# A fused decoder layer on one core: order of the additions, weight loads and first feed-forward products between cross-attention and the feed-forward part

## The chip, the cores and the metric

The kernel runs on one NeuronCore of a Trainium2 chip as one launch. The metric is the device time of that launch in microseconds (us). Three runs of the kernel before gave 2944.31, 2949.00 and 2949.56 us; the median, 2949.0 us, is the time before. Engines are called by the names of the profile: PE (TensorE), DVE (VectorE), ACT (ScalarE), POOL (GpSimd), SP (SyncE, which here only issues DMAs).

## The reference, cut to what matters

One decoder layer is applied to 512 prompt tokens and to 8 x 4 sample tokens, which share the weights. All values are float32.

```
x = x + concat(stick_breaking_attention, gated_delta_net) @ w_out
hx = rmsnorm(x, norm_x_g)
xq = rmsnorm(hx @ w_xq per head, x_q_norm_g)            # 4 heads of 128
attn = softmax(xq . mem_k / sqrt(128))                  # 256 memory tokens
x = x + (attn @ mem_v) @ w_xo                           # w_xo: 512 x 2048
hf = rmsnorm(x, norm_ffn_g)
gate, up = split(hf @ w_gate_up)                        # 2048 x 2*5632
x = x + (silu(gate) * up) @ w_down                      # 5632 x 2048
```

The prompt attends to memory keys and values computed from `mem_prompt`, the samples to cached ones (`cache_mem_k`, `cache_mem_v`). The change lies at the seam between the last two additions: the product with `w_xo`, the norm `norm_ffn_g`, and the first products with `w_gate_up`.

## The kernel before

**Layout.** Features lie on the partitions. The token vector `x` is 16 tiles (blocks) of 128 features x 544 tokens; the 544 tokens are worked on in two halves of 272 columns. A product of float32 numbers is made of three matmuls: both factors are split into a high and a low part (`wh`/`wl` for a weight, `xh`/`xl` or the two parts of `pr` for the tokens), and high x high, high x low and low x high are added in PSUM. The high part is made by a cast on ACT, the low part by a subtraction on DVE.

**Cross-attention** (`cross`, L1522). Side work for the sample tokens (`cross_sample`, L1434) runs between the projections: it loads cached keys (`xk`, L1456) in two halves and then cached values (`xv`, L1465) in four groups of four tiles, all on SP. Then the product with `w_xo` runs in two parts, one for each half of the tokens. Each part has 16 blocks, each block 12 matmuls (L1570) into a PSUM tile `mm` (two of them exist). The weights of one block (four 128 x 128 tiles, 256 KB) are loaded by one DMA (`wxo`, L1546, through `weights`, L191) into a raw tile `wr` (three exist), cast (L203) and subtracted (L204). The first six blocks are kept for part 1; the other ten are loaded again, two blocks ahead. After a block's matmuls DVE adds the PSUM tile to `x` (L1573).

**The operands of the feed-forward part.** Two blocks of `x` make a `Pair`. `Pair.first` and `Pair.second` multiply by the norm's gain (`gain`, partly on POOL, L1635, partly on ACT, L1637), `sums` makes four differences and sums on DVE (L1666 to L1669, tiles `v`), and `make` splits them into parts `pr` (cast L1640 on ACT, subtraction L1641 on DVE). In parallel `Stats` squares `x` (ACT, L266) and accumulates `acc` on POOL (L267). `Stats.rstd` (L270) then sums `acc` over the partitions with a matmul (L277) into PSUM and makes `rstd2` out of it and of `r1`, the earlier norm's factor (L281, L282, then a logarithm and an exponential on ACT). `aux` is one PSUM tile here, so the second half's matmul waits until DVE has read the first half's.

**The feed-forward part** uses a scheme of seven products in place of eight. One product (`Ffn.product`, L2006) is 24 matmuls of 272 columns; the kernel calls it a tick. What every engine does is written out by hand: `Work.at(tick, place, do)` enters a step in a list, and `Work.run` (L1702) emits each tick's steps by their place. Steps of the ticks below 0, and those of ticks 0 to 4 with a place under 70, get a higher priority in the scheduler, so that they may move ahead of the part before. There are two sets of PSUM banks for gate and up. One set (`gu_banks[0]`) shares its PSUM space with `mm`, the other one (`gu_banks[1]`) has its own.

`FirstGateUp` (L1798) runs the first pair of hidden columns as eight products in ticks 0 to 7. Its raw weight tiles (512 KB each, `raw`) are loaded by SP, cast on ACT (L1785) and subtracted on DVE (L1789). `open` (L2015) starts four accumulators with one matmul each. `scale` calls `rstd` for `rstd2`, both halves, in tick 5. `unscale` (L2020 to L2030) runs in tick 20: it transposes `rstd2`, multiplies `r1` by it (L2029) and takes the reciprocal of all 128 x 544 elements (L2030), which POOL uses from tick 41 on.

Each engine executes its instructions in the order in which they stand; the order comes from the scheduler, which goes by the steps' priorities.

Of the kernel before, what the change touches and what calls it, by code (L numbers as in the profile page):

```python
# [12 lines left out]
ALU = mybir.AluOpType  # L13
# [239 lines left out]
class Stats:  # L253
# [16 lines left out]
    def rstd(self, name, scale=None):  # L270

        c, nc = self.c, self.c.nc
        r = c.cst.tile([P, T], F32, tag="rstd", name=name, bufs=2)
        for h in range(2):
            cols = slice(h * HT, (h + 1) * HT)
            ps = c.aux()
            nc.tensor.matmul(ps[:, :HT], c.ones, self.acc[:, cols], start=True, stop=True)  # L277
            if scale is None:
                rsq(c, r[:, cols], ps[:, :HT], 1.0 / D)
                continue  # L280
            nc.vector.tensor_mul(r[:, cols], scale[:, cols], scale[:, cols])  # L281
            nc.vector.scalar_tensor_tensor(r[:, cols], r[:, cols], D * EPS, ps[:, :HT], ALU.mult, ALU.add)  # L282
            rsq(c, r[:, cols], r[:, cols], 1.0 / D, eps=c.zero)
        return r
# [1148 lines left out]
def cross_sample(c, qs, outs, scale, tiles):  # L1433
# [14 lines left out]
    yield 0.3, 2.5  # L1448
    for h2 in range(2):

        def load(b, i):
            if h2 or b >= 2:
                t = c.tt("xk")[:, :512]
            else:
                t = c.pb.tile([P, 4, P], F32, tag="wh", name="xk", bufs=XO_KEPT).rearrange("p k m -> p (k m)")
            nc.sync.dma_start(  # L1456
                t.rearrange("p (a h d) -> p a h d", a=2, h=2), c.cache_mk[0, b, :, h2 * 2 : h2 * 2 + 2].rearrange("(a p) h d -> p a h d", p=P)
            )
            return t

        ps = yield from sample_logits(c, f, h2 * 2, load, 1, ps if h2 else None, h2 * 256)

    def loadv(b, j):
        t = c.act.tile([P, T], F32, tag=("ah", "al")[b % 2], name="xv", bufs=KD)[:, :512]
        nc.sync.dma_start(t, c.cache_mv[0, b, j * P : (j + 1) * P].rearrange("p h d -> p (h d)"))  # L1465
        return t


    values = [[loadv(i // 2 * 4 + b, i % 2) for b in range(4)] for i in range(3)]
# [22 lines left out]
    for half in range(2):  # L1492
        ps = c.aux()
        for j in range(2):
# [7 lines left out]
            if not half and not j:  # L1502
                values.append([loadv(4 + b, 1) for b in range(4)])
# [17 lines left out]
def cross(c, acts, st, x, side):  # L1521
# [24 lines left out]
    def wxo(m):  # L1546
        if m < len(kept):
            return kept[m]
        if len(kept) == XO_KEPT:
            return weights(c, c.w_xo, 0, 4, m * P)  # L1550
        kept.append(weights(c, c.w_xo, 0, 4, m * P, kept=True))
        return kept[-1]

    for part in range(2):
# [4 lines left out]
        ahead = [wxo(m) for m in range(2)]  # L1559
        for m in range(KD):  # L1560
            ps = c.mm()
            if m + 2 < KD:
                with c.tc.high_priority(PRIO):
                    ahead.append(wxo(m + 2))
# [7 lines left out]
            with c.tc.high_priority(100):  # L1572
                nc.vector.tensor_add(x[m][:, cols], x[m][:, cols], ps[:, 0, :HT])  # L1573
# [222 lines left out]
class FirstGateUp:  # L1796
# [3 lines left out]
    def __init__(self, f):  # L1800
        self.f, self.c, self.cols, self.a, self.hi, self.lo = f, f.c, (0, HID), {}, {}, {}
        at = f.work.at
        (A, B, C, _), (A1, B1, C1, _) = f.gu_banks
# [156 lines left out]
class Ffn:  # L1960
# [4 lines left out]
    def __init__(self, c, pairs, st, r1):  # L1965
# [13 lines left out]
        at(0, 1, self.open)  # L1979
        at(5, 35, self.scale)  # L1980
        at(20, 35, self.unscale)
        self.xq = c.dram.tile([KD, P, T], F32, name="xq")
# [27 lines left out]
    def open(self):  # L2010

        g = self.first
        for k in range(2):
            for b in self.gu_banks[k][1:3]:
                self.c.nc.tensor.matmul(b, g.hi["11"][:, :P], self.pairs[0].op[1][0], start=True, stop=True, skip_group_check=True)  # L2015

    def scale(self):
        self.rr = self.st.rstd("rstd2", self.r1)

    def unscale(self):  # L2020
# [9 lines left out]
        nc.vector.reciprocal(self.r1, self.r1)  # L2030
# [333 lines left out]
```

## Time and profile before

| what | value |
|---|---|
| runs, median (lowest, highest) | 2949.0 us (2944.31, 2949.56) |
| profiled execution, its own time | 2948.57 us |
| its span (first to last instruction) | 2946.9 us |
| PE busy | 2861.5 us, 97% |
| DVE busy | 2101.8 us, 71% |
| ACT busy | 1490.2 us, 51% |
| POOL busy | 737.4 us, 25% |
| mean granted clock of PE | 0.992 of full speed |

The profile is one execution. Its start times count from the first instruction. Busy shares are averages over very different stages. A row that names an idle time in brackets says what ended that wait. A group's idle time counts only where its engine is one that the others wait for. The granted clock stands as a share of the full 2.4 GHz; 0.50 is the lower of its two levels, 1.2 GHz.

The seam lies between about 1438 and 1594 us of the span: samples and `w_xo` up to 1504, the first products and the operands up to 1541, the reciprocal at 1585.

### The profile page before, as it was taken

The numbers are of one execution on the slowest core, as the hardware profiler recorded it, in microseconds if no ns is written. First come the engines' busy times: TensorE is split into PE (matmuls) and PEld (weight loads), VectorE is DVE, ScalarE is ACT, GpSimd is POOL, SyncE is SP. The second block draws the span as 40 slices with busy tenths as digits, with TensorE's granted clock in tenths as the row PEclk, the third lists the DMA queues.
The fourth block names the chain that finished last, engine by engine and source line by source line (L and its number), as shares of the span: only waits on it lengthen the run. The fifth ranks groups of instructions, "written<-read, shape, count | busy, mean of one in ns | idle before, by whom it ended". The sixth has DMA issues, their size and how long they took to land. (4 is left out here: it accounts for less than half of the span.)

```text
span 2946.9 us, 57039 instructions
## 1 busy us (share of the span) xinstructions
PE 2861.5 (97%) x22146; PEld 2770.9 (94%) x22146; DVE 2101.8 (71%) x3317; ACT 1490.2 (51%) x2836; POOL 737.4 (25%) x923
## 2 busy tenths in 40 slices
PE   8999999999999999999989999999999999999998
PEld 7999999889889989999779999999999999999998
DVE  5776775655555564436677888888888887888886
ACT  4544443445555574425654444444444446655675
POOL 3211212313212100003232343433334334211200
PEclk9999999999999999999989999999999999999999
DMA  7323223454453685432543554555455548966653
GB/s 220 92 76 93 78 83 92 132 155 124 141 166 104 183 263 155 143 114 76 161 143 113 169 168 149 163 161 158 150 165 169 150 133 259 273 197 202 186 174 98
DMA packets 640423, 444.39 MB, mean 151 GB/s; under 512 B 36412, under 2 KB 566665, under 8 KB 640153
## 3 DMA queue, kind: packets, MB, share of 16 engines
q1 hardware_dynamic: 608328, 386.31, 44.7%
q0 software_dynamic: 22176, 42.90, 4.7%
q10 hardware_dynamic: 9648, 11.54, 1.1%
q8 instruction: 174, 2.85, 0.4%
q14 instruction: 97, 0.79, 0.1%
HBM read 360.07 MB, written 80.58 MB: 150 GB/s over the span
## 5 line engine op out<-in xcount | busy, mean ns | idle before, releaser
L2006 PE MATMUL gu<-pr,wh 128*128 128x272 f32 x4944 | 675.9, 289 | 4.8 <-DVE u L1745 4.8
L2006 PEld LDWEIGHTS gu<-pr,wh 128*128 128x128 f32 x4944 | 645.1, 190 | 5.2 <-issue 5.0
L215 PE MATMUL mm<-ah,wh 128*128 128x272 f32 (+1 forms) x2464 | 538.7, 299 | 5.8 <-ACT ah L328 4.6
L215 PE MATMUL mm<-al,wh 128*128 128x272 f32 (+1 forms) x2464 | 524.3, 291 | 0.7 <-DVE al L246 0.7
L215 PE MATMUL mm<-ah,wl 128*128 128x272 f32 (+1 forms) x2464 | 515.7, 290 | 0.1
L1891 PE MATMUL bank<-pr,wh 128*128 128x272 f32 x2464 | 466.3, 289 | 1.9 <-ACT bank L1919 1.9
L215 PEld LDWEIGHTS mm<-ah,wh 128*128 128x128 f32 (+1 forms) x2464 | 391.9, 189 | 29.2 <-issue 8.5
L204 DVE TENSOR_TENSOR wl<-wr,wh 128x512 fp32r<-128x512 f32 (+1 forms) x366 | 262.3, 720 | 200.9 <-ACT wh L203 190.5
L215 PEld LDWEIGHTS mm<-al,wh 128*128 128x128 f32 (+1 forms) x2464 | 389.9, 188 | 5.4 <-issue 2.0
L203 ACT CAST wh<-wr 128x512 fp32r<-128x512 f32 (+1 forms) x366 | 224.3, 616 | 332.4 <-PE mm L215 272.5
L1891 PEld LDWEIGHTS bank<-pr,wh 128*128 128x128 f32 x2464 | 385.9, 188 | 4.0 <-ACT bank L1919 3.6
L215 PEld LDWEIGHTS mm<-ah,wl 128*128 128x128 f32 (+1 forms) x2464 | 386.4, 188 | 2.5 <-issue 0.5
L2006 PE MATMUL gu<-pr,wl 128*128 128x272 f32 x2472 | 361.9, 289 | 0.0
L1891 PE MATMUL bank<-pr,wl 128*128 128x272 f32 x1232 | 354.4, 288 | 0.0
L2006 PEld LDWEIGHTS gu<-pr,wl 128*128 128x128 f32 x2472 | 331.3, 189 | 0.0
L1789 DVE TENSOR_TENSOR wl<-sum,wh 128x1024 fp32r<-128x1024 f32 x172 | 220.2, 1280 | 78.9 <-ACT wh L1785 78.8
L1891 PEld LDWEIGHTS bank<-pr,wl 128*128 128x128 f32 x1232 | 232.1, 188 | 0.0
L1785 ACT CAST wh<-sum 128x1024 fp32r<-128x1024 f32 x172 | 180.4, 1049 | 80.5 <-PE gu L2006 47.3
L1789 DVE TENSOR_TENSOR wl<-raw,wh 128x1024 fp32r<-128x1024 f32 x133 | 202.7, 1526 | 17.8 <-ACT wh L1785 15.5
L1785 ACT CAST wh<-raw 128x1024 fp32r<-128x1024 f32 x133 | 139.8, 1051 | 101.8 <-PE gu L2006 95.0
L2076 POOL DMA_DIRECT2D pr<-hT x154 | 81.9, 549 | 256.0 <-PE bank L1891 227.1
L1778 DVE TENSOR_TENSOR sum<-raw,sum 128x1024 f32<-128x1024 f32 x86 | 136.4, 1586 | 0.9
(535 smaller groups left out, 4384.9 us busy)
## 6 DMA issues: line engine op xcount, KB each, us to landing
raw<-in_w_gate_up SPq DMA_DIRECT2D x176, 512.0 KB
wr<-in_w_in SPq DMA_DIRECT2D x108, 512.0 KB
raw<-in_w_down SPq DMA_DIRECT2D x176, 256.0 KB
hT<-hs SPq DMA_DIRECT2D x154, 272.0 KB
pr<-hT POOLq DMA_DIRECT2D x154, 272.0 KB, 7.0
page<-in_cache_sb_k SPq DMA_DIRECT2D x128, 128.0 KB
page<-in_cache_sb_v SPq DMA_DIRECT2D x64, 256.0 KB
wr<-in_w_out SPq DMA_DIRECT2D x32, 512.0 KB
```

Of the source, the lines that this page charges most:

```text
L203: nc.scalar.copy(hi[:, :m, :n], raw[:, k : k + m, :n])
L204: nc.vector.tensor_sub(lo[:, :m, :n], raw[:, k : k + m, :n], hi[:, :m, :n].bitcast(F32))
L215: c.nc.tensor.matmul(ps[:n, h, :HT], l[:, :n], r[:, h * HT : (h + 1) * HT], start=first and i == 0, stop=last and i == 2,)
L1778: self.f.c.nc.vector.tensor_sub(self.a[q], self.a[x], self.a[y])
L1785: self.f.c.nc.scalar.copy(self.hi[q], self.left(q))
L1789: self.f.c.nc.vector.tensor_sub(self.lo[q], self.left(q), self.hi[q].bitcast(F32))
L1891: self.c.nc.tensor.matmul(self.c.bank[bank][:, o], t[x][:, s, i * P : (i + 1) * P], pairs[i].op[q][r], start=new and not (i or n), stop=se ...
L2006: self.c.nc.tensor.matmul(bank, w[:, i * P : (i + 1) * P], self.pairs[i].op[q][r], start=start and n == 0, stop=n == 23, skip_group_check= ...
L2076: self.c.nc.gpsimd.dma_start(t, self.hT[2 * g + pair, :, max(0, 2 * n - 1) + k])
```

## The change

1. `cross_sample` loads the first group of four cached values between the two halves of the keys, the other three groups after them.
2. `wxo` loads two blocks with one DMA (512 KB, 13 loads in place of 26); casts and subtractions stay one per block. Six blocks are kept as before.
3. The addition to `x` is emitted with `high_priority(500)` in place of 100.
4. `FirstGateUp` uses the two bank sets the other way round: its first products write the set that does not share space with `mm`. `open` is split into one tick per set.
5. `rstd` is split by halves: `rstd2`'s first half is made in tick 5, the second in tick 6.
6. The reciprocal leaves `unscale`; it is made in four pieces of 128 x 136 in ticks 21 to 24, place 75.

```diff
 class Stats: def rstd(self, name, scale=None):
-        for h in range(2):
-            cols = slice(h * HT, (h + 1) * HT)
...
+        for h in range(2):
+            self.half(r, h, scale)
+        return r
+
+    def half(self, r, h, scale):
+        cols = slice(h * HT, (h + 1) * HT)
+        ps = c.aux()
+        nc.tensor.matmul(ps[:, :HT], c.ones, self.acc[:, cols], start=True, stop=True)
...
+        nc.vector.tensor_mul(r[:, cols], scale[:, cols], scale[:, cols])
+        nc.vector.scalar_tensor_tensor(r[:, cols], r[:, cols], D * EPS, ps[:, :HT], ALU.mult, ALU.add)
+        rsq(c, r[:, cols], r[:, cols], 1.0 / D, eps=c.zero)

 def cross_sample
+    values = []
+    def some(i):
+        values.append([loadv(i // 2 * 4 + b, i % 2) for b in range(4)])
     for h2 in range(2):
+        if h2:
+            some(0)
...
         ps = yield from sample_logits(c, f, h2 * 2, load, 1, ps if h2 else None, h2 * 256)
-    values = [[loadv(i // 2 * 4 + b, i % 2) for b in range(4)] for i in range(3)]
+    some(1)
+    some(2)

 def cross
     def wxo(m):
         if m < len(kept):
-            return kept[m]
-        if len(kept) == XO_KEPT:
-            return weights(c, c.w_xo, 0, 4, m * P)
-        kept.append(weights(c, c.w_xo, 0, 4, m * P, kept=True))
-        return kept[-1]
+            return kept[m : m + 2]
+        keep = len(kept) < XO_KEPT
+        parts = [[(c.pb if keep else c.w).tile([P, 4, P], F32R, tag=x, name=x, bufs=XO_KEPT if keep else 4) for x in ("wh", "wl")] for _ in range(2)]
+        raw = c.w.tile([P, 8, P], F32, tag="wr", name="wr", bufs=3).rearrange("p (k i) m -> p k i m", i=2)
+        nc.sync.dma_start(raw.rearrange("p k i m -> p k (i m)"), c.w_xo[: 4 * P, m * P : (m + 2) * P].rearrange("(k p) m -> p k m", p=P))
+        for i, (hi, lo) in enumerate(parts):
+            nc.scalar.copy(hi, raw[:, :, i])
+            nc.vector.tensor_sub(lo, raw[:, :, i], hi.bitcast(F32))
...
-        ahead = [wxo(m) for m in range(2)]
+        ahead = wxo(0)
         for m in range(KD):
             ps = c.mm()
-            if m + 2 < KD:
+            if m % 2 == 0 and m + 2 < KD:
                 with c.tc.high_priority(PRIO):
-                    ahead.append(wxo(m + 2))
+                    ahead = ahead + wxo(m + 2)
...
-            with c.tc.high_priority(100):
+            with c.tc.high_priority(500):
                 nc.vector.tensor_add(x[m][:, cols], x[m][:, cols], ps[:, 0, :HT])

 class FirstGateUp
-        (A, B, C, _), (A1, B1, C1, _) = f.gu_banks
+        (A1, B1, C1, _), (A, B, C, _) = f.gu_banks

 class Ffn
-        at(0, 1, self.open)
-        at(5, 35, self.scale)
+        for i in range(2):
+            at(i, 1, lambda i=i: self.open(1 - i))
+        self.rr = c.cst.tile([P, T], F32, tag="rstd", name="rstd2", bufs=2)
+        for h in range(2):
+            at(5 + h, 35, lambda h=h: st.half(self.rr, h, r1))
         at(20, 35, self.unscale)
+        for i in range(4):
+            at(21 + i, 75, lambda i=i: c.nc.vector.reciprocal(r1[:, i * (T // 4) :][:, : T // 4], r1[:, i * (T // 4) :][:, : T // 4]))
...
         nc.vector.tensor_mul(self.r1, self.r1, self.rr)
-        nc.vector.reciprocal(self.r1, self.r1)
```

SP's queue at the end of cross-attention (`wr` is a load of `w_xo`, `raw` one of `w_gate_up`), before:

```order
L1456 DMA xk<-in_cache_mem_k 128x2x256 x11
L198 DMA wr<-in_w_xo 128x4x128 x2
L1465 DMA xv<-in_cache_mem_v 128x512
L198 DMA wr<-in_w_xo 128x4x128
L1465 DMA xv<-in_cache_mem_v 128x512 x11
L198 DMA wr<-in_w_xo 128x4x128 x3
L1465 DMA xv<-in_cache_mem_v 128x512 x2
L198 DMA wr<-in_w_xo 128x4x128
L1465 DMA xv<-in_cache_mem_v 128x512 x2
L198 DMA wr<-in_w_xo 128x4x128 x3
L2000 DMA raw<-in_w_gate_up 128x8x128 x5
L198 DMA wr<-in_w_xo 128x4x128 x3
```

and now:

```order
L1564 DMA wr<-in_w_xo 128x4x256 x7
L1473 DMA xk<-in_cache_mem_k 128x2x256 x3
L1564 DMA wr<-in_w_xo 128x4x256
L1473 DMA xk<-in_cache_mem_k 128x2x256 x3
L1455 DMA xv<-in_cache_mem_v 128x512 x4
L1473 DMA xk<-in_cache_mem_k 128x2x256 x8
L1564 DMA wr<-in_w_xo 128x4x256
L1455 DMA xv<-in_cache_mem_v 128x512 x8
L1564 DMA wr<-in_w_xo 128x4x256 x3
L1455 DMA xv<-in_cache_mem_v 128x512 x4
L1564 DMA wr<-in_w_xo 128x4x256
L2024 DMA raw<-in_w_gate_up 128x8x128 x14
```

The last three loads of `w_xo` stood behind five loads of `w_gate_up`; now none does. Four loads of cached values stand ahead of the last eight loads of keys.

PE at the end of part 1 of the product with `w_xo` (`mm`; `gu_...` are the accumulators of gate and up), before:

```order
L1570 MATMUL mm<-xh,wh 128x272
L1570 MATMUL mm<-xl,wh 128x272
L1570 MATMUL mm<-xh,wl 128x272
L2015 MATMUL gu_18773<-pr,wh 128x272
L2015 MATMUL gu_18777<-pr,wh 128x272
L2015 MATMUL gu_18782<-pr,wh 128x272
L2015 MATMUL gu_18786<-pr,wh 128x272
L2006 MATMUL gu_18772<-pr,wh 128x272 x16
L2006 MATMUL gu_18772<-pr,wl 128x272 x8
L2006 MATMUL gu_18787<-pr,wh 128x272 x16
```

and now, in block 9 of part 1 and, behind the left-out rows, at its end:

```order
L1589 MATMUL mm<-xh,wh 128x272
L1589 MATMUL mm<-xl,wh 128x272
L2038 MATMUL gu_18756<-pr,wh 128x272
L2038 MATMUL gu_18760<-pr,wh 128x272
L2030 MATMUL gu_18761<-pr,wh 128x272 x16
L1589 MATMUL mm<-xh,wl 128x272
...
L1589 MATMUL mm<-xh,wl 128x272
L2030 MATMUL gu_18761<-pr,wl 128x272 x8
L2038 MATMUL gu_18747<-pr,wh 128x272
L2038 MATMUL gu_18751<-pr,wh 128x272
L2030 MATMUL gu_18746<-pr,wh 128x272 x16
L2030 MATMUL gu_18746<-pr,wl 128x272 x8
```

Eighteen matmuls of the first product stand behind the 110th of part 1's 192 matmuls, 82 ahead of its end; its other eight stand right behind that end.

DVE around the last addition to `x` (`wl<-raw` are low parts of the first `w_gate_up` tiles), before:

```order
L1573 TENSOR_TENSOR x_16553<-x_16553,mm 128x272
L1666 TENSOR_TENSOR v<-v 128x272
L1667 TENSOR_TENSOR v<-v 128x272
L1789 TENSOR_TENSOR wl<-raw,wh 128x1024 x3
L1668 TENSOR_TENSOR v<-v 128x272
L1573 TENSOR_TENSOR x_16680<-x_16680,mm 128x272
L1669 TENSOR_TENSOR v<-v 128x272
```

and now:

```order
L1592 TENSOR_TENSOR x_16553<-x_16553,mm 128x272
L1688 TENSOR_TENSOR v<-v 128x272
L1660 TENSOR_TENSOR pr<-v,pr 128x544
L1592 TENSOR_TENSOR x_16680<-x_16680,mm 128x272
L1808 TENSOR_TENSOR wl<-raw,wh 128x1024 x3
L1660 TENSOR_TENSOR pr<-v,pr 128x272
```

The three large subtractions moved from ahead of the last addition to right behind it. Further on, the reciprocal (L2030) stood between the multiplication of L2029 and the addition `u` (L1745); now `u` follows that multiplication at once, and the four pieces stand 6, 10, 13 and 15 rows behind `u`.

## Rows read from the trace of the kernel before

**Rows 1.** The page: PE's share of the span, and its granted clock by 40 slices.

```profile
PE 2861.5 (97%) x22146; PEld 2770.9 (94%) x22146; DVE 2101.8 (71%) x3317; ACT 1490.2 (51%) x2836; POOL 737.4 (25%) x923
PEclk9999999999999999999989999999999999999999
```

**Rows 2.** Waits of PE, 1400 to 1600 us: total, times, longest.

```profile
PE aux L277 <- DVE rstd L282: 5.1, 1, 5.1
PE gu L2006 <- DVE u L1745: 4.8, 1, 4.8
PE gu L2015 <- DVE x L1573: 4.4, 1, 4.4
PE mm L1570 <- ACT wh L203: 3.1, 1, 3.1
...
PE aux L1498 <- DMA xv<-in_cache_mem_v: 2.2, 1, 2.2
...
PE mm L1570 <- DVE x L1573: 0.8, 2, 0.6
```

**Rows 3.** Busy time by stretch: sum, PE, PEld, DVE, ACT, POOL, clock, DMA share, GB/s.

```profile
1470.50:1504.20 33.70, 29.80 (x192) 28.47 (x192) 21.84 (x48) 16.40 (x32) 12.92 (x11) 0.85 0.67 206
1494.50:1501.50 7.00, 4.96 (x20) 4.74 (x21) 2.71 (x5) 3.59 (x7) 4.44 (x4) 0.60 0.56 193
1508.40:1533.90 25.50, 20.77 (x150) 20.37 (x150) 18.31 (x31) 12.82 (x28) 14.05 (x13) 0.92 0.18 56
1534.40:1539.00 4.60, 4.55 (x18) 4.35 (x19) 3.07 (x5) 3.65 (x7) 0.00 (x0) 0.50 0.09 20
1588.80:1593.60 4.80, 4.80 (x21) 4.80 (x22) 4.01 (x5) 1.44 (x2) 0.00 (x0) 0.50 0.32 91
1593.60:1620.00 26.40, 26.40 (x208) 26.40 (x207) 20.29 (x21) 10.80 (x15) 6.20 (x4) 0.98 0.35 106
```

**Rows 4.** SP's timeline: start, length, line, transfer, count of the issues.

```profile
1481.43 6.88 SPq L2000 DMA_DIRECT2D raw<-in_w_gate_up  x5
1488.42 4.64 SPq L198 DMA_DIRECT2D wr<-in_w_xo  x3
```

**Rows 5.** ACT's timeline: two casts of weights and what they waited for.

```profile
1486.03 1.05 ACT L1785 CAST wh<-raw 128x1024 fp32r<-128x1024 f32 x1 [1.10 <-DMA raw<-in_w_gate_up]
1495.87 0.62 ACT L203 CAST wh<-wr 128x512 fp32r<-128x512 f32 x1 [2.75 <-DMA wr<-in_w_xo]
```

**Rows 6.** DVE's timeline from 1504 us on, and around the reciprocal.

```profile
1504.24 3.50 DVE L1789 TENSOR_TENSOR wl<-raw,wh 128x1024 fp32r<-128x1024 f32 x3 [0.31 <-PE mm L1570]
...
1508.00 0.43 DVE L1573 TENSOR_TENSOR x<-x,mm 128x272 f32<-128x272 f32 x1
...
1520.39 0.44 DVE L1668 TENSOR_TENSOR v<-v 128x272 f32<-128x272 f32 x1
...
1521.11 1.02 DVE L1669 TENSOR_TENSOR v<-v 128x272 f32<-128x272 f32 x1
...
1533.87 0.44 DVE L282 SCALAR_TENSOR_TENSOR rstd<-rstd,aux 128x272 f32<-128x272 f32 x1
...
1584.77 3.55 DVE L2030 RECIPROCAL rstd<-rstd 128x544 f32<-128x544 f32 x1
1588.23 0.38 DVE L1745 TENSOR_TENSOR u<-gu,e 128x272 f32<-128x272 f32 x1
```

**Rows 7.** PE's timeline from the last `w_xo` matmul to the eighth product.

```profile
1503.91 0.28 PE L1570 MATMUL mm<-xh,wl 128*128 128x272 f32 x1
...
1525.72 2.16 PE L2006 MATMUL gu<-pr,wh 128*128 128x272 f32 x16
1527.72 1.17 PE L2006 MATMUL gu<-pr,wl 128*128 128x272 f32 x8
...
1534.45 1.25 PE L277 MATMUL aux<-acc,ones 128*128 128x272 f32 x2 [5.11 <-DVE rstd L282]
...
1540.62 1.66 PE L2006 MATMUL gu<-pr,wh 128*128 128x272 f32 x12
```

More of the change, by code (lines that the diff above doesn't have):

```diff
@@ L270, in rstd @@
     def rstd(self, name, scale=None):
-        c, nc = self.c, self.c.nc
-        r = c.cst.tile([P, T], F32, tag="rstd", name=name, bufs=2)
-        for h in range(2):
-            cols = slice(h * HT, (h + 1) * HT)
[L276 to L284, printed above, removed]
+        r = self.c.cst.tile([P, T], F32, tag="rstd", name=name, bufs=2)
+        for h in range(2):
+            self.half(r, h, scale)
+        return r
+    def half(self, r, h, scale):
+        c, nc = self.c, self.c.nc
+        cols = slice(h * HT, (h + 1) * HT)
+        ps = c.aux()
+        nc.tensor.matmul(ps[:, :HT], c.ones, self.acc[:, cols], start=True, stop=True)
+        if scale is None:
+            rsq(c, r[:, cols], ps[:, :HT], 1.0 / D)
+            return
+        nc.vector.tensor_mul(r[:, cols], scale[:, cols], scale[:, cols])
+        nc.vector.scalar_tensor_tensor(r[:, cols], r[:, cols], D * EPS, ps[:, :HT], ALU.mult, ALU.add)
+        rsq(c, r[:, cols], r[:, cols], 1.0 / D, eps=c.zero)
 def load_x(c, wload):
@@ L1448, in cross_sample, with loadv @@
     yield 0.3, 2.5
+    def loadv(b, j):
+        t = c.act.tile([P, T], F32, tag=("ah", "al")[b % 2], name="xv", bufs=KD)[:, :512]
+        nc.sync.dma_start(t, c.cache_mv[0, b, j * P : (j + 1) * P].rearrange("p h d -> p (h d)"))
+        return t
+    values = []
+    def some(i):
+        values.append([loadv(i // 2 * 4 + b, i % 2) for b in range(4)])
     for h2 in range(2):
+        if h2:
+            some(0)
         def load(b, i):
@@ L1461, in cross_sample @@
         ps = yield from sample_logits(c, f, h2 * 2, load, 1, ps if h2 else None, h2 * 256)
[L1463 to L1466, printed above, removed]
-    values = [[loadv(i // 2 * 4 + b, i % 2) for b in range(4)] for i in range(3)]
+    some(1)
+    some(2)
     tiles[0] = c.tt = lambda name: c.t.tile([P, T], F32, tag="t", name=name, bufs=c.nt)
@@ L1502, in cross_sample @@
             if not half and not j:
-                values.append([loadv(4 + b, 1) for b in range(4)])
+                some(3)
             yield 0.5, 0.2
@@ L1547, in wxo @@
         if m < len(kept):
-            return kept[m]
-        if len(kept) == XO_KEPT:
-            return weights(c, c.w_xo, 0, 4, m * P)
-        kept.append(weights(c, c.w_xo, 0, 4, m * P, kept=True))
-        return kept[-1]
+            return kept[m : m + 2]
[6 more added lines that the diff above has]
+            nc.vector.tensor_sub(lo, raw[:, :, i], hi.bitcast(F32))
+        out = [[(hi[:, k, :], lo[:, k, :]) for k in range(4)] for hi, lo in parts]
+        if keep:
+            kept.extend(out)
+        return out
     for part in range(2):
@@ L2008, in product, with open @@
             )
-    def open(self):
+    def open(self, k):
         g = self.first
[L2013 to L2018, printed above, removed]
+        for b in self.gu_banks[k][1:3]:
+            self.c.nc.tensor.matmul(b, g.hi["11"][:, :P], self.pairs[0].op[1][0], start=True, stop=True, skip_group_check=True)
     def unscale(self):
```

## The prediction

> **What bounds the kernel now.** First the page: PE is busy 97% of the span, and the granted clock is in its upper tenth in every slice but one, at the seam the change touches [rows 1]. So the kernel is bound by PE's matmuls, and the change, which takes no matmul away, can only win what PE loses by waiting or by a low clock. Second, the list of PE's waits: at the seam five large ones stand, 2.2 us for cached values, 3.1 for a cast of `w_xo`, 4.4 for the last addition to `x`, 5.1 for `rstd2`, and 4.8 for `u` behind the reciprocal [rows 2]. With 19.5 us these are nearly all that PE waits for there. Third, the table by stretch: behind the waits PE's clock falls. The stretches at 1494.5, 1534.4 and 1588.8 us were granted 0.60, 0.50 and 0.50 [rows 3], which loses 7.0 x 0.40 + 4.6 x 0.50 + 4.8 x 0.50 = 7.5 us. The ceiling is thus 27.1 us (0.9% of the time). From 1594 us on PE is busy throughout (26.40 of 26.40 in the stretch to 1620 [rows 3]), so what is won at the seam should reach the end.
>
> I follow the gain along the places where PE must wait, in the profile's own times; at full clock 16 matmuls take 2.00 us (1525.72 to 1527.72 [rows 7]), 0.125 us each.
>
> **Start of part 1, and the cached values (edit 1).** Part 1 starts at 1470.5. Of what is ahead of it only the 2.2 us for `xv` goes; with the first group loaded earlier I take all of it, 1468.3. The price: eight loads of keys now stand behind four more loads. Four tiles of 128 x 512 float32 are 1.05 MB; at the 206 GB/s of the nearest stretch [rows 3] they are 5.1 us late at worst. PE's list has no wait for a key now [rows 2], so I take nothing. Bounds: 2.2 us won to 2.9 lost.
>
> **End of the `w_xo` product (edits 2 and 4).** Its 192 matmuls ended at 1503.91 + 0.28 = 1504.2 [rows 7], 33.7 us after the start at a clock of 0.85. Two things stretched it. SP issued five `w_gate_up` loads (512 KB each) at 1481.43 and only then, at 1488.42, the last `w_xo` loads [rows 4]; the first of these was cast at 1495.87, after ACT had waited 2.75 us for it [rows 5]. That is PE's 3.1 us, and the clock fell behind it. Now all `w_xo` loads stand ahead of the raw ones, so the wait goes. What is late next is the raw weights: 18 matmuls of the first product now stand ahead of part 1's last 82. Raw loads were issued when PE was through block 5; that is 72 matmuls into the part, the new ones stand at 110, so PE comes there 38 x 0.125 = 4.8 us after the issue. In the rows the first raw tile is cast at 1486.03 to 1487.08, 5.6 us after the issue [rows 4, 5]. I take 1.0 us of wait there. So the end is 1468.3 + 192 x 0.125 + 0.8 (waits for additions, kept [rows 2]) + 18 x 0.125 + 1.0 = 1496.4, with 18 matmuls of the first product done. The number of loads, 13 for 26, I price at nothing: the wait comes from their place in the queue, and I see no wait that hangs on their issue.
>
> **Last addition and first products (edits 3 and 4).** The last addition stood behind 3.50 us of large subtractions and began at 1508.00 [rows 6], and because the first bank set shared PSUM space with `mm`, PE waited 4.4 us. Now the first set is free and the addition stands ahead of the subtractions. The 3.5 us do not vanish: the first product's last eight matmuls need the first of them, 0.5 + 1.2 = 1.7 us after the end. From there 24 x 6 + 4 - 18 = 130 matmuls stand ahead of the first `rstd2` matmul: 16.3 us. With 1.4 us for operands of the later pairs, PE is there at 1496.4 + 1.7 + 16.3 + 1.4 = 1515.8, against 1528.7 before.
>
> **`rstd2` (edit 5) is the next gate.** PE is 13 us earlier, but DVE's chain (operands of pairs 4 to 7, then L282) need not be. From the last addition, 1508.4, to L282, 1533.9, DVE was busy 18.3 of 25.5 us [rows 3]. Behind the addition now stand 3.5 us of subtractions more and some 1.6 less (what moved ahead of it, and the second half of `rstd2`): 20.2 us. Unbroken but for 4 us of waits, the chain takes 24.3; with the same idle time and the 3.5 us all added, 29.4. I take the middle, 27: L282 begins at 1496.5 + 27 = 1523.5, before 1533.87. In the meantime PE does one product more, since the second half now stands a product later: it reaches the second matmul at 1515.8 + 0.3 + 3.0 = 1519.1 and waits until 1524. This is the largest wait that stays. Before, PE's matmul began at 1534.45, 0.14 us after L282's end [rows 6, 7], and took some 0.6; so the eighth product begins at 1524.7. Before, it began at 1540.62, with the seventh ahead of it at half clock [rows 7]. If the clock falls behind the new wait as it did then, that loses 4.6 x 0.50 = 2.3 us again [rows 3]. Half of it counted: 1525.8 against 1540.62, **14.8 us** won. Bounds: 18.6 with the short chain and no fall, 11.3 with the long chain and the fall.
>
> **Reciprocal (edit 6).** `u` began at 1588.23, behind 3.55 us of reciprocal begun at 1584.77 [rows 6]. It now begins where the reciprocal did: **3.4 us** won of the 4.8, and 1.4 us stay for `rstd2`'s transposes and the multiplication ahead of `u`. Whether the clock falls behind so short a wait the rows leave open (it fell to 0.50 behind 4.8 us, a loss of 2.4 [rows 3]); half of it counted, **1.2 us**. The pieces cost 3.55 us and three starts more. A subtraction takes 0.44 us for 272 columns and 3.50/3 = 1.17 for 1024 [rows 6]; the line through both has 0.18 us at no columns, my estimate of a start: 4.1 us in all, on DVE in ticks 21 to 24. DVE was busy 20.29 of 26.40 us from 1593.6 on [rows 3], which leaves 2.8 us free in four ticks of 3.0. What is over, 1.3 us, is the upper bound of the price, and nothing the lower one, if DVE is ahead of PE by as much; I charge 0.4. POOL's use of the result is 17 ticks away.
>
> **Sum.** 14.8 + 3.4 + 1.2 - 0.4 = 19.0 us. The profiled execution took 2948.57 (span 2946.9 and 1.7 around it), 0.4 under the median: 2948.57 - 19.0 + 0.4 = **2930.0 us**, 0.6% faster. All bounds at their good ends give 18.6 + 3.4 + 2.4 = 24.4, 2924.6; at their bad ends 11.3 + 3.4 - 1.3 = 13.4, 2935.6, and with the keys 5.1 us late, 2940.7.
>
> **A rule that speaks against it.** Rows first: between 1508 and 1534 us a subtraction of 272 columns takes 0.44 us alone (1520.39) and 1.02 beside POOL (1521.11) [rows 6]; POOL was busy 14.05 us there [rows 3]. The Trainium skill (SBUF — State Buffer, section "SBUF: two separate sides") says that VectorE instructions with two SBUF inputs and GpSimd instructions share one port pair, held by whoever came first for the whole instruction. By that rule the two would take turns; the trace agrees in part only, since 18.31 + 14.05 = 32.4 us of work lie in 25.5 [rows 3].
>
> **The rivals.**
> - *DVE and POOL take turns on the packed chain.* Where the chain is squeezed from 25.5 us, their overlap shrinks. 20.2 less the 2.3 us by which five subtractions are stretched now is 17.9, with POOL's 14.05 [rows 3] 32.0 in place of 27: five us later at `rstd2`, **2935**. For it: the stretched subtractions. Against it: the overlap of 7 us that the trace has. Chance 0.18.
> - *The chain keeps its dates; nothing but the reciprocal is won.* ACT, POOL and DVE feed each other, and waits for pairs 5 to 7 appear in ticks 4 to 6, where PE is earlier. Then only 3.4 + 1.2 remain, with up to 1 us of what PE gained ahead: **2943 to 2945**. For it: DVE idles 7 of 25.5 us, so its pace is set elsewhere. Against it: the chain starts with the last addition, which is 11 us earlier. Chance 0.13.
> - *PE stands in order behind a late weight (slower).* The 18 matmuls stand ahead of 82 that the additions and the whole chain wait for, and SP, in order too, issues the raw loads only behind the last `w_xo` load. If that one cannot go out before its tile is free, the raws are late with it. Before, the last `w_xo` loads were through SP at 1488.42 + 4.64 = 1493.1 [rows 4]. Raws issued then are cast 5.6 us later, at 1498.7, while PE comes to the 18 matmuls at 1468.3 + 0.8 + 110 x 0.125 = 1482.9: a wait of 15.8 us in place of 1.0, and a fall of the clock behind it, 2.4: 2930 + 14.8 + 2.4 = 2947. It decides (slower than before) from a wait of some 18 us: issues twice as long, for loads twice as large, add 4.6, 2952; and if the first raw lands only with all five (2.6 MB at 206 GB/s, 12.7 us) 7 more, **2959**. Against it: with two blocks in a load, three raw tiles reach six blocks ahead, so the last load's tile is free once the weights of blocks 8 and 9 are cast, and those take the place of part 0's last ones. Chance of slower than before 0.07.
> - *The loads only change places.* Keys come late in place of values, 5.1 us at worst: **2935**, within the range and counted with the forecast. That the change does not move what it says the order of the instructions excludes.
>
> **How the numbers follow.** Forecast 0.62, with a range of its own from 2924 to 2938, turns 0.18, dates kept 0.13, late weight 0.07. A measurement of this kernel can tell about 0.2%, 5.9 us, from no change: faster means under 2943.1, slower over 2954.9. The second rival's times begin at the first of these lines and count as the same. Faster 0.62 + 0.18 = 0.80, same 0.13, slower 0.07. The range reaches from 2921, the ceiling's 27.1 us all won, to 2943, where the chain that keeps its dates begins.
>
> **What would show it.** Right: no wait for `x` at `open` and none for `wh` of `w_xo`; first `gu` matmuls near 1482, `w_xo` over near 1496; PE's largest wait at the seam for `rstd2`, some 4 to 5 us, ended near 1524; `u` begins some 0.8 us after PE's transposes, PE waits under 2 us. Wrong: a wait over 3 us at the 18 early matmuls, waits for `pr` in ticks 4 to 6, or waits for `wl` in ticks 21 to 24.

## The result, and the profile after

The changed kernel took 2927.58 us (median of 4 runs, 2925.6 to 2930.64) against 2946.65 us for the kernel before: a ratio of 0.9936, 95% interval [0.9919, 0.9953], 19.1 us faster. Forecast were 2930.0 us and 19.0 us, the latter from a median of 2949.0 before; a fourth run brought that median to 2946.65. A second series of the unaltered changed kernel gave 2927.63 us, ratio 0.9942 [0.9928, 0.9956]. The profiled execution took 2926.94 us with a span of 2925.2.

The page after, busy shares and PE's granted clock, answers to [rows 1]: PE is busy 9 us less in a span that is 22 us shorter, and the slice with the low clock is gone.

```profile
PE 2852.4 (98%) x22146; PEld 2762.6 (94%) x22146; DVE 2104.0 (72%) x3320; ACT 1489.1 (51%) x2836; POOL 739.1 (25%) x923
PEclk9999999999999999999999999999999999999999
```

PE's waits of the changed kernel from 1400 to 1600 us answer to [rows 2]:

```profile
PE gu L2030 <- ACT pr L1659: 3.3, 3, 2.5
PE aux L970 <- DMA xk<-in_cache_mem_k: 2.2, 1, 2.2
PE gu L2030 <- ACT gu L1779: 2.0, 1, 2.0
PE gu L2030 <- issue: 1.8, 1, 1.8
PE gu L2030 <- DVE u L1764: 1.3, 1, 1.3
PE aux L709 <- DVE part L667: 0.9, 2, 0.6
...
PE gu L2038 <- ACT wh L1804: 0.5, 1, 0.5
```

Of the five waits of before four are gone, those for `xv`, for a cast of `w_xo`, for `x` and for `rstd2`; the one for `u` went from 4.8 to 1.3. New at the seam are 3.3 us for operands `pr`, 2.0 for a copy on ACT, 1.8 for the first product's low weights (put down to "issue"; DVE finished them just before). Ahead of it 0.9 us for `part` are new, DVE's split of cached keys. The 2.2 us for a key, ahead of the seam too, are no longer than what they replace. At the same transposition of `xk` the kernel before waited for DVE:

```profile
PE aux L967 <- DVE sm L1381: 2.0, 1, 2.0
```

Where the gain arises is read from PE's timeline. The two executions are already 1.71 us apart where the seam begins, at the first matmul of `rstd1`, so I count from there. The changed kernel:

```profile
1349.69 1.08 PE L281 MATMUL aux<-acc,ones 128*128 128x272 f32 x4
...
1467.08 0.52 PE L1589 MATMUL mm<-xh,wh 128*128 128x272 f32 x2 [0.70 <-ACT xh L1528]
...
1482.30 0.52 PE L2038 MATMUL gu<-pr,wh 128*128 128x272 f32 x2 [0.50 <-ACT wh L1804]
1482.66 2.17 PE L2030 MATMUL gu<-pr,wh 128*128 128x272 f32 x16
...
1494.86 0.28 PE L1589 MATMUL mm<-xh,wl 128*128 128x272 f32 x1
1496.92 1.25 PE L2030 MATMUL gu<-pr,wl 128*128 128x272 f32 x8 [1.77 <-issue]
...
1512.58 1.02 PE L2030 MATMUL gu<-pr,wh 128*128 128x272 f32 x2 [2.50 <-ACT pr L1659]
...
1518.83 0.62 PE L281 MATMUL aux<-acc,ones 128*128 128x272 f32 x2
...
1523.92 2.35 PE L2030 MATMUL gu<-pr,wh 128*128 128x272 f32 x16
...
1535.67 2.91 PE L2030 MATMUL gu<-pr,wh 128*128 128x272 f32 x16 [1.96 <-ACT gu L1779]
...
1570.36 0.60 PE L970 MATMUL aux<-ident,rstd 128*128 128x128 f32 x4
...
1572.82 2.25 PE L2030 MATMUL gu<-pr,wh 128*128 128x272 f32 x16 [1.31 <-DVE u L1764]
...
1578.92 2.16 PE L2030 MATMUL gu<-pr,wh 128*128 128x272 f32 x16
```

and three rows of the kernel before that [rows 7] does not have:

```profile
1351.40 0.85 PE L277 MATMUL aux<-acc,ones 128*128 128x272 f32 x3
...
1582.78 0.60 PE L967 MATMUL aux<-ident,rstd 128*128 128x128 f32 x4
...
1597.59 1.65 PE L2006 MATMUL gu<-pr,wh 128*128 128x272 f32 x12
```

The last row of either view is the second product behind the one that waits for `u`; the text calls it "the second product behind `u`".

| us from the first matmul of `rstd1` | before | after | won so far |
|---|---|---|---|
| part 1 starts | 119.1 | 117.4 | 1.7 |
| last `w_xo` matmul | 152.5 | 145.2 | 7.3 |
| first `rstd2` matmul | 177.3 | 169.1 | 8.2 |
| eighth product | 189.2 | 174.2 | 15.0 |
| transposes, tick 20 | 231.4 | 220.7 | 10.7 |
| second product behind `u` | 246.2 | 229.2 | 17.0 |

The reader is to see two things: the gain falls by 4.3 us between the eighth product and tick 20, and the jump over `u` is 6.3 us. (In the second profile of the changed kernel, further down, the fall is 2.9 us.) The rest of the 21.7 us between the two spans lies outside the seam (1.7 ahead, 3.0 behind), and the runs of one kernel spread over 5 us.

Much of the gain is clock. Busy time times (1 - granted clock), in pieces of 5 us from part 1's start to the second product behind `u`, sums to 10.9 us before and 3.2 after; that stretch is 127.1 and 111.8 us long.

### The profile page after: what moved, and what is told of

Same layout as the page of the kernel before. It is cut to its first block, busy times and chain, and to the rows that moved or that the text cites. A ratio compares the mean times of both kernels' runs of the same rounds, so it can differ in the third digit from the quotient of the medians.

```text
span 2925.2 us, 57002 instructions
## 1 busy us (share of the span) xinstructions
PE 2852.4 (98%) x22146; PEld 2762.6 (94%) x22146; DVE 2104.0 (72%) x3320; ACT 1489.1 (51%) x2836; POOL 739.1 (25%) x923
## 5 line engine op out<-in xcount | busy, mean ns | idle before, releaser
L2030 PE MATMUL gu<-pr,wh 128*128 128x272 f32 x4944 | 672.8, 289 | 7.1 <-ACT pr L1659 3.3
L2030 PEld LDWEIGHTS gu<-pr,wh 128*128 128x128 f32 x4944 | 640.8, 189 | 8.9 <-ACT pr L1659 3.9
L204 DVE TENSOR_TENSOR wl<-wr,wh 128x512 fp32r<-128x512 f32 (+1 forms) x340 | 244.6, 724 | 183.2 <-ACT wh L203 174.6
L203 ACT CAST wh<-wr 128x512 fp32r<-128x512 f32 (+1 forms) x340 | 208.3, 615 | 316.4 <-PE mm L215 275.2
L2030 PE MATMUL gu<-pr,wl 128*128 128x272 f32 x2472 | 362.0, 289 | 2.0 <-issue 1.8
L2030 PEld LDWEIGHTS gu<-pr,wl 128*128 128x128 f32 x2472 | 330.4, 189 | 2.4 <-issue 2.0
L1808 DVE TENSOR_TENSOR wl<-raw,wh 128x1024 fp32r<-128x1024 f32 x133 | 204.0, 1535 | 15.3 <-ACT wh L1804 13.5
```

The costliest lines, as they stand in the source:

```text
L203: nc.scalar.copy(hi[:, :m, :n], raw[:, k : k + m, :n])
L204: nc.vector.tensor_sub(lo[:, :m, :n], raw[:, k : k + m, :n], hi[:, :m, :n].bitcast(F32))
L1808: self.f.c.nc.vector.tensor_sub(self.lo[q], self.left(q), self.hi[q].bitcast(F32))
L2030: self.c.nc.tensor.matmul(bank, w[:, i * P : (i + 1) * P], self.pairs[i].op[q][r], start=start and n == 0, stop=n == 23, skip_group_check= ...
```

## The experiments

Each of the first six undoes one edit; the seventh makes one alone. The table has the two stretches of each profile, with the clock loss (busy time times (1 - granted clock), pieces of 10 us ahead of part 1, of 5 behind) in brackets; "second" is the second product behind `u`. The ratio is to the kernel before in the same rounds.

| kernel | `rstd1` to part 1 | part 1 to second | median us | ratio, interval |
|---|---|---|---|---|
| before | 119.1 (1.3) | 127.1 (10.9) | 2943.5 to 2946.7 | |
| changed | 117.4 (1.3) | 111.8 (3.2) | 2927.58 | 0.9936 [0.9919, 0.9953] |
| changed, again | 118.3 (2.6) | 110.1 (1.6) | 2927.63 | 0.9942 [0.9928, 0.9956] |
| without edit 1 | 113.9 (0.0) | 111.9 (3.0) | 2925.79 | 0.9936 [0.9920, 0.9953] |
| without edit 2 | 117.1 (0.0) | 117.9 (6.3) | 2930.30 | 0.9950 [0.9933, 0.9966] |
| without edit 3 | 118.5 (2.6) | 110.3 (1.2) | 2926.45 | 0.9939 [0.9923, 0.9956] |
| without edit 4 | 116.2 (0.0) | 115.8 (4.3) | 2926.83 | 0.9940 [0.9919, 0.9961] |
| without edit 5 | 119.8 (2.6) | 113.2 (4.1) | 2928.79 | 0.9948 [0.9931, 0.9964] |
| without edit 6 | 116.5 (1.3) | 119.7 (8.5) | 2931.64 | 0.9954 [0.9938, 0.9971] |
| edit 2 alone | 114.8 (1.3) | 124.0 (8.9) | 2937.82 | 0.9981 [0.9971, 0.9991] |
| copy first | 116.8 (1.3) | 110.3 (1.6) | 2924.61 | 0.9933 [0.9916, 0.9949] |
| no edit 1, copy first | 114.3 (0.0) | 110.6 (3.1) | 2923.78 | 0.9931 [0.9918, 0.9945] |
| and gains on ACT | 114.9 (0.3) | 109.5 (4.4) | 2923.47 | 0.9930 [0.9917, 0.9944] |

Single medians of kernels 2 to 4 us apart do not tell them apart; the stretches tell more. Once the clock loss is taken off, the two profiles of the changed kernel agree behind part 1 (108.6 and 108.5 us). Ahead of it the seven profiles with both edit 1 and edit 2 spread over 2 us (115.2 to 117.2).

### Without edit 1

```diff
-        if h2:
-            some(0)
...
+    some(0)
     some(1)
     some(2)
```

> The changed kernel with edit 1 alone undone: all cached values are loaded behind the keys again. Measured from the first matmul of rstd1 (the seam's start) to the second product behind u, the stretch was 246.2 us before and 229.2 with the change. Theory (the prediction's step): PE's wait for cached values comes back, part 1 starts 1.7 to 2.2 us later and all behind it is late by as much: 231.2, 2929.5 us. Rival (the loads only change places): the wait of 2.2 us for a key, new in the changed kernel, goes in exchange: 229.2, 2927.6 us.

Both missed: part 1 started at 113.9 us, 3.5 earlier. No wait for values came back, and the wait for a key is 1.0 instead of 2.2:

```profile
PE aux L970 <- DMA xk<-in_cache_mem_k: 1.0, 1, 1.0
```

Of the 3.5 us 1.3 are clock, which has nothing to do with the edit (last section). With the clock loss taken off, the seven profiles that load `w_xo` by two blocks and have edit 1 start part 1 at 115.2 to 117.2 us, the four without it at 113.5 to 114.6. Edit 1 thus costs some 1.9 us in the profiles and wins nothing there; the times don't tell (both ratios are 0.9936). The wait for a key does not carry that cost alone: 2.0 us of it stand in the last kernel of the table too, which has no edit 1. What every profile with edit 1 has and none without is the 0.9 us for `part`. That its four loads of values make the second half of the keys late, and `part` with them, is argued from SP's order and not shown.

### Without edit 2

```diff
-        raw = c.w.tile([P, 8, P], F32, tag="wr", name="wr", bufs=3).rearrange("p (k i) m -> p k i m", i=2)
...
+        if len(kept) == XO_KEPT:
+            return weights(c, c.w_xo, 0, 4, m * P)
+        kept.append(weights(c, c.w_xo, 0, 4, m * P, kept=True))
+        return kept[-1]
```

> The changed kernel with edit 2 alone undone: w_xo in 26 loads of one block. Three of them then stand behind five raw loads in SP's queue again. Theory (place in the queue): ACT waits for one of the three, PE for its cast, some 3 us, and the clock falls behind it, 2 to 3 us; the stretch of 229.2 us becomes 234 to 235, the time 2933 us. Rival (the other edits took that wait away, since the additions now stand earlier and PE has 18 matmuls to do): within 1 us of 229.2, 2927.6 us.

The theory held in size, 235.0 us for the whole stretch, but not in shape. SP's timeline has three `w_xo` loads behind five raw ones again, as in [rows 4]:

```profile
1477.02 6.82 SPq L2016 DMA_DIRECT2D raw<-in_w_gate_up  x5
1483.94 4.48 SPq L198 DMA_DIRECT2D wr<-in_w_xo  x3
```

and PE waits less long, but three times:

```profile
PE gu L2022 <- issue: 2.5, 1, 2.5
...
PE mm L1581 <- DVE x L1584: 1.1, 1, 1.1
PE mm L1581 <- ACT wh L203: 1.0, 1, 1.0
```

Behind part 1's start 6.1 us are lost, 3.1 of it clock (7.8 and 4.7 against the second profile of the change). The edit changes number, size and place of the loads at once; that the place does it is read from these rows.

### Without edit 3

```diff
-            with c.tc.high_priority(500):
+            with c.tc.high_priority(100):
```

> The changed kernel with edit 3 alone undone: additions at priority 100. Only the last addition moves, behind three large subtractions. Theory (the chain of operands starts with the last addition): the operands of pairs 5 to 7 and rstd2 are 3.5 us late, and since PE already waits for them, so is PE: stretch 232.7, 2931 us. Rival (DVE does the same sum of work, and the first product's low weights come 1.7 us earlier, which saves PE's wait there): 228 to 229.5, 2927 us.

The rival held in its number: 110.3 us behind part 1, no loss that the profile can tell. PE waits 2.3 us for the last addition, now ahead of the second bank set's opening, and 1.9 instead of 3.3 for operands:

```profile
PE gu L2038 <- DVE x L1592: 2.3, 1, 2.3
...
PE gu L2030 <- ACT pr L1659: 1.9, 1, 1.9
PE gu L2030 <- DVE wl L1808: 1.9, 2, 1.7
```

One wait stands for the other. The rival's second reason failed, since the wait for the first low weights is still 1.7 us. Its first one, that DVE has the same work to do in either order, fits DVE's rows:

```profile
1499.38 0.42 DVE L1592 TENSOR_TENSOR x<-x,mm 128x272 f32<-128x272 f32 x1
...
1522.27 0.44 DVE L286 SCALAR_TENSOR_TENSOR rstd<-rstd,aux 128x272 f32<-128x272 f32 x1
```

Counted from part 1's start, the last addition is 4.6 us later than in the changed kernel (32.7 against 28.1; there it began at 1495.18), and L286 is no later (55.5 against 55.8).

### Without edit 4

```diff
-        (A1, B1, C1, _), (A, B, C, _) = f.gu_banks
+        (A, B, C, _), (A1, B1, C1, _) = f.gu_banks
...
-            at(i, 1, lambda i=i: self.open(1 - i))
+            at(i, 1, lambda i=i: self.open(i))
```

> The changed kernel with edit 4 undone: first products in the bank set that shares PSUM space with the w_xo product. Theory (with the additions early, the chain of operands, and not the banks, sets PE's pace in ticks 3 to 5): the w_xo product ends 2.3 us earlier without the 18 matmuls inside it, PE waits about 1 us for the last addition, and most of what is lost is taken out of the waits for operands: stretch 229 to 231, 2928.5 us. Rival (the banks carried the gain): the wait of 4.4 us at the opening matmuls is back in part, with a fall of the clock behind it: 233 to 235, 2932.5 us.

Between the two: 232.0 us, 4.0 lost behind part 1, 2.9 of it without the clock (5.7 and 3.0 against the second profile of the change). The times don't tell (0.9940 and 0.9936). The 18 matmuls no longer hide in the `w_xo` product, and the wait at the opening is only 0.5 us. Most of the wait of 4.4 us before [rows 2] was thus the late addition and not the banks alone. What the early matmuls had hidden turned into waits for operands, 5.6 us in place of 3.3, and into 1.6 us for earlier additions inside the product:

```profile
PE gu L2030 <- ACT pr L1659: 5.6, 3, 2.8
...
PE mm L1589 <- DVE x L1592: 1.6, 2, 1.4
...
PE gu L2038 <- DVE x L1592: 0.5, 1, 0.5
```

### Without edit 5

```diff
-            at(5 + h, 35, lambda h=h: st.half(self.rr, h, r1))
+            at(5, 35, lambda h=h: st.half(self.rr, h, r1))
```

> The changed kernel with edit 5 alone undone: both halves of rstd2 in tick 5. Stretch (first matmul of rstd1 to the second product behind u) 246.2 us before, 229.2 with the change. Theory: PE stands at the second half's matmul from 169.4 until DVE has read the first half's (173.6), 4 us and a fall of the clock, in place of a product there; but its later waits for operands (0.8 us) and for ACT's copy at 186.0 (2.0 us and a fall of the clock) go, since rstd2 is early against PE again: stretch 230 to 232, 2930 us. Rival (the halves are worth the whole wait, as the prediction had it: a product of 3.0 us and 2.3 us of clock): 233 to 235, 2932.5 us.

The wait for `rstd2` is back at 4.0 us and the one for the copy is gone, as the theory had it. The loss behind part 1 is 1.4 us against the first profile of the change and 3.1 against the second (111.8 and 110.1 with the edit, 113.2 without), some 0.5 of it without the clock. (The whole stretch, 233.0, lies in the rival's range, but 2.4 us of it are ahead of part 1, where the edit changes nothing.)

```profile
PE aux L281 <- DVE rstd L286: 4.0, 1, 4.0
```

So edit 5 mostly moves a wait: PE does a product sooner, and comes 2 us too early to the copy on ACT.

### Without edit 6

```diff
-        for i in range(4):
-            at(21 + i, 75, lambda i=i: c.nc.vector.reciprocal(...))
...
+        nc.vector.reciprocal(self.r1, self.r1)
```

> The changed kernel with edit 6 alone undone: the reciprocal in one piece ahead of u. Theory: u is 3.4 us later, PE waits 4.8 us in place of 1.3, and the clock falls behind the long wait, 2 us more: stretch 234 to 235, 2933 us. Rival (the pieces cost DVE as much in ticks 21 to 24, where PE then waits): 229 to 231, 2928.5 us.

The theory held, and the loss was larger: 236.2 us (its time, 2931.64, is less than the 2933 expected). PE's timeline of this kernel:

```profile
1569.63 0.60 PE L970 MATMUL aux<-ident,rstd 128*128 128x128 f32 x4
...
1575.61 3.96 PE L2028 MATMUL gu<-pr,wh 128*128 128x272 f32 x16 [4.85 <-DVE u L1764]
...
1584.05 2.17 PE L2028 MATMUL gu<-pr,wh 128*128 128x272 f32 x16
```

From the transposes to the second product behind `u` it takes 14.4 us, the change 8.6 (1570.36 to 1578.92), before 14.8. The edit is worth 5.9 to 6.3 us there: 3.5 of wait and the rest a product at half clock. With the edit PE has no wait in ticks 21 to 24, so the pieces cost nothing.

### Edit 2 alone

> The kernel before with edit 2 alone: w_xo in 13 loads, all ahead of the raw ones. Theory (the place in SP's queue is what made ACT and PE wait): the wait of 3.1 us for the cast goes, with the fall of the clock behind it, 2.8 us; all later waits keep their length: stretch 246.2 - 6 = 240, 2940.5 us. If the wait of 2.2 us for cached values goes too, since fewer loads stand among theirs (undoing edit 1 did not bring it back): 238. Rival (the chain of operands to rstd2 sets the date, whatever PE does ahead of it): the wait for rstd2 grows by what is won, 245 to 246, 2946 us.

The edit is that of `wxo` in the diff above, in the kernel before. The theory held with its second clause: 238.8 at the row that it names, 2937.8 us. The wait of 3.1 us for the cast is gone, and the one of 2.2 us for cached values too, without edit 1. Which of number, size and place of the loads did the latter is not shown. The large waits behind keep their length; that for `rstd2` grows by 0.4:

```profile
PE aux L277 <- DVE rstd L282: 5.5, 1, 5.5
PE gu L2014 <- DVE u L1753: 4.8, 1, 4.8
PE gu L2023 <- DVE x L1581: 4.4, 1, 4.4
```

### The copy first

```diff
-            at(5 + i * 3 // 4, 72, lambda i=i: pairs[i].make(3))
+            at((5, 5, 6, 7, 9, 9, 10, 11)[i], 64 if i == 3 else 72, lambda i=i: pairs[i].make(3))
```

> The changed kernel with the last casts and subtractions of the operands moved in the hand-written order (pair 3 ahead of the first silu, pairs 4 and 5 from tick 8 to 9, pairs 6 and 7 a tick later). Theory (PE's new wait of 2.0 us at 186.0 is one for ACT's queue: two casts of 0.6 us stand ahead of the copy that PE needs): the wait falls under 0.8 us and the clock does not fall behind it: stretch 226 to 227.5, 2925 us. Rival (the wait is one for rstd2, through the silu that stands ahead of the copy): the wait keeps over 1.5 us, stretch 228.5 to 229.5, 2927.5 us.

Two casts of 0.6 us stood ahead of the copy in ACT's queue; in the changed kernel:

```profile
1534.15 1.19 ACT L1659 CAST pr<-v 128x544 fp32r<-128x544 f32 x2
1535.24 0.38 ACT L1779 COPY gu<-gu 128x272 f32<-128x272 f32 x1
```

With these moved the wait fell from 2.0 to 0.3, and the clock did not fall behind it. But pair 7, a tick later, came late from DVE:

```profile
PE gu L2030 <- DVE pr L1660: 2.0, 2, 1.6
...
PE gu L2030 <- ACT gu L1779: 0.3, 1, 0.3
```

The theory is right on the cause of the wait: it is ACT's order, and not `rstd2` itself. That anything is won is not shown: without the clock loss the stretch behind part 1 is 108.7 us against 108.6 and 108.5, and the second profile of the change, with the wait, had no fall of the clock behind it either (110.1 us).

### The change again, and two versions that go further

The first is unaltered.

> The changed kernel once more, unaltered, beside the next two. It shows how far one profile of the same program lies from another. From the first matmul of rstd1 to part 1's start the profiles of kernels that are alike there lay between 116.2 and 119.8 us, from there to the second product behind u the change took 111.8. Expected: 116 to 120, and 111 to 113; time 2926 to 2928.5 us.

Part 1 starts at 118.3 us, 110.1 us from there (111 expected at least), 2927.63 us. The waits are those of the first profile to 0.3 us, but for the 0.5 at the opening, which is missing.

> The changed kernel with edit 1 undone and the last operands moved as in the run that put the copy first, but with pair 7 in tick 10 together with pair 6. Theory (edit 1 delays the keys by more than it wins on the values; the copy waits in ACT's queue; pair 7 was late on DVE): part 1 starts at 113.5 to 115 in place of 117.4, from there 108.5 to 110 in place of 111.8 us; 2921 to 2923 us, 4 to 6 us under the change in the same rounds. Rival (the early start at part 1 in two profiles without edit 1 was chance, as the spread of 3.6 us among like kernels could have it): part 1 at 116 to 120, time 1 to 2.5 us under the change.

```diff
 # edit 1 undone as above, and
+            at((5, 5, 6, 7, 9, 9, 10, 10)[i], 64 if i == 3 else 72, lambda i=i: pairs[i].make(3))
```

Part 1 started at 114.3, as the theory said. The stretch behind it took 110.6 us (110 expected at most), with two falls of the clock (3.1 us); without them 107.5 against 108.6. The time, 2923.78 us, is over the 2921 to 2923 of the theory, and 3.85 under the change in the same rounds, where 4 was the least that it allowed; the intervals of the two ratios overlap.

> As the run before it, and for pairs 5 to 7 both gains are made on ACT (0.75 us each) in place of one on POOL (1.65 to 1.84). Theory (PE's wait of 2.5 us for operands in tick 4 comes from POOL, where gains and sums of squares stand in turn): the wait falls under 1 us and its fall of the clock goes, 2 to 4 us less than the run before it; 2918 to 2920.5 us. Rival (ACT is as full there as POOL, and the chain only changes its engine): within 1 us of the run before it.

```diff
-            self.gain(self.v[k], k, slice(0, T), k == 0)
+            self.gain(self.v[k], k, slice(0, T), k == 0 and self.blocks[0] < 10)
```

The long wait for operands shrank from 2.5 us to two of 0.8 and 0.4, and the stretch without its clock loss to 105.1 us. That is 2.4 less than the run before it, as the theory said of the work; and behind that wait the clock no longer fell. But it fell elsewhere (0.50 over the first 5 us of part 1, 0.83 over the 10 us behind its end; 4.4 us in all), and the times, 2923.47 and 2923.78, are equal, as the rival said. Both versions are faster than the kernel before; that they beat the change is likely and not shown.

## Why the prediction was right, and where it was not

The mechanism held at the `w_xo` product and at the reciprocal, not at the gate between them. The gain forecast was 19.0 us and the gain measured 19.1, and that they agree so well is luck: in the profile the seam won 17.0. A loss of 4.3 us was not foreseen, the reciprocal won 2.1 us more than forecast, and the time is 2.4 us off because the median before had come down by nearly as much.

**Start of part 1.** 2.2 us forecast, 1.7 found, and from another cause. The two-block loads took the wait for `xv` away (edit 2 alone: 114.8 against 119.1; the wait is 2.2 of the 4.3 us, the rest is not explained). Edit 1, to which I gave it, costs some 1.9. The bound "late keys" had that sign right; what shows is the wait for `part`.

**End of the `w_xo` product.** Forecast 1496.4; measured 1494.86 + 0.28, with the 1.7 us of the early offset 1496.8. No wait for a cast of `w_xo` is left; the 18 early matmuls began at 1482.30 and had waited 0.5 us where I took 1.0. Edit 2 is shown as the cause by undoing it and by making it alone; that it works through the place in SP's queue is argued from the order of the loads. Pricing the number of loads at nothing was not borne out: the wait for cached values ahead of part 1 went with that edit as well, by which side of it is not shown.

**Last addition.** The wait of 4.4 us is gone, and 1.8 us stand at the first low weights (1.7 forecast). That the addition's place as such matters was not borne out: undoing edit 3 costs nothing that can be told, and `rstd2` is no later for it. With the additions early, the banks put back bring only 0.5 us of that wait (without edit 4).

**`rstd2` as the next gate.** This is the step that failed. I had PE at the first `rstd2` matmul at 1515.8 and standing 4 to 5 us at the second. It came at 1518.83, 4.7 us later with the offset counted. Of that, 1.4 us are a longer wait for operands (2.8; 1.4 were foreseen, for which the rows gave no source) and 1.6 the fall of the clock behind it. That wait, in tick 4, and 0.8 us more in tick 6 are a sign that the prediction itself had named for being wrong. At the second matmul PE did not wait at all. But DVE's chain, the other side of the same gate, was sized well: 27 us forecast from the last addition to L286, 27.2 found, with DVE busy 20.8 (20.2 forecast). The reason given, that the chain starts with the last addition, does not hold: without edit 3 the addition came 4.6 us later and L286 did not. The row answers to the third of [rows 3]:

```profile
1495.60:1522.80 27.20, 22.09 (x150) 20.77 (x151) 20.82 (x31) 11.46 (x25) 13.92 (x13) 0.94 0.32 100
```

PE was held back by operands instead of by `rstd2`, and the eighth product began as forecast: 15.0 us won, 14.8 forecast. That is luck in part, since the sum had 4 to 5 us of wait at `rstd2` and half a fall of the clock in it, and neither came.

**What I did not see.** With the eighth product sooner behind `rstd2`, a copy on ACT that stands behind the silu and two casts became a gate: 2.0 us of wait and a fall of the clock of 1.6, of the 4.3 us lost by tick 20. My sum took it that what is won at the eighth product is kept; the profile before had no wait between it and tick 20, and I read that as slack.

**Reciprocal.** 4.2 us forecast (3.4, half of the clock's 2.4, less 0.4); 6.3 found. The wait fell to 1.3 us as I had it, the clock fell by nothing behind it, and the pieces (0.98 to 1.00 us each, 4.0 in all where 4.1 were estimated) were free:

```profile
1572.80:1578.90 6.10, 6.08 (x48) 6.10 (x49) 6.07 (x9) 2.15 (x3) 0.88 (x1) 1.00 0.42 121
```

**The rivals.** Turns of DVE and POOL: the row at 1495.60 has 20.82 + 13.92 = 34.7 us of work in 27.2, an overlap of 7.5 us, no less than before. The rule of the Trainium skill (SBUF — State Buffer, "SBUF: two separate sides"), by which one waits for the whole instruction of the other, does not give this chain. As far as the profile's spans on POOL can tell, a subtraction took its 0.44 us in the midst of a multiplication of POOL:

```profile
1508.38 1.83 POOL L1654 TENSOR_SCALAR v<-x,gains 128x544 f32<-128x544 f32 x1
...
1509.20 0.44 DVE L1660 TENSOR_TENSOR pr<-v,pr 128x272 fp32r<-128x272 f32 x1 [0.51 <-ACT pr L1659]
```

Others of its size were stretched, to 0.83 to 1.00 us. The prediction's "0.44 us alone" (1520.39) was misread: in the kernel before POOL was at work there too.

```profile
1519.16 1.84 POOL L1635 TENSOR_SCALAR v<-x,gains 128x544 f32<-128x544 f32 x1
```

The chain that keeps its dates: wrong in its size, since L286 came 9.3 us earlier (11.0 less the offset of 1.7), right in its sign, waits for `pr` in ticks 4 and 6. Late weights: the raw loads went out at 1476.52, behind block 5 of part 1, as before.

**Sums and the ceiling.** The five waits add up to 19.6 us and not 19.5, and the long end of the chain is 25.5 + 3.5 = 29.0 and not 29.4, which would move its middle from 27 to 26.6. The ceiling of 27.1 was none. It counted 7.5 us of clock, but the pieces of 5 us have 10.9: falls at the start of part 1 and behind the wait for `x` were put at nothing. Rows of the kernel before:

```profile
1470.47:1475.47 5.00, 5.00 (x27) 4.95 (x28) 2.00 (x8) 1.79 (x7) 1.91 (x2) 0.66 0.14 56
1508.58:1513.58 5.00, 5.00 (x28) 5.00 (x29) 3.20 (x7) 2.80 (x6) 1.62 (x2) 0.66 0.55 168
```

## What to carry to other kernels

When a wait is taken away, follow the next reader of the same chain as far as the gain is to be kept: where the profile shows no wait, the slack is unknown, not large. A wait of a few microseconds on PE can cost more than its length, where the clock falls behind it; here 7.7 of 15.3 us won behind part 1 were clock. And look at what a load stands behind in its queue: half as many, twice as large loads, ahead of another tensor's, removed two waits, one of them for cached values. Undo every edit by itself: of six, one here (edit 1) cost time in the profiles, and one (edit 3) did nothing that they can tell.

## What the hardware showed that was not expected

The granted clock falls in some executions of the same instructions and not in others. The edits move nothing in the 20 us behind the first matmul of `rstd1`; and the two waits of PE that come first there, 1.6 and 0.84 us, are the same in all 13 profiles to 0.03 us. Yet eight of the 13 were granted 0.83 in its second ten microseconds, a loss of 1.3 us of matmul time, and five 1.00. (Not all of it is lost: without the fall PE then waits 0.56 us for DVE.) The changed kernel, and the one without edit 1:

```profile
1359.69:1369.69 10.00, 7.55 (x47) 7.03 (x46) 9.89 (x11) 4.32 (x12) 10.00 (x8) 0.83 0.04 11
```

```profile
1356.97:1366.97 10.00, 6.99 (x50) 6.22 (x49) 9.90 (x11) 4.32 (x12) 10.00 (x8) 1.00 0.06 18
```

The same holds behind the wait of 2.0 us for the copy, which seven profiles have: the clock fell behind it in three of them (in the first profile of the changed kernel to 0.66 over five microseconds) and not in four, the second profile of the changed kernel among these. Behind the waits of 4.8 us for `u` it fell each time (before, without edit 6, edit 2 alone). A few such falls, of 1.3 to 1.7 us each, are as large as the effects that single edits have here; a comparison of two profiles has to take them off first.
